# Layer 0's gate and up projections by seven products of halves, with weight factors in quarter units

## The chip, the cores and the metric

The kernel runs on one core of a Trainium2 chip. The metric is device time in microseconds (us), the median of several executions; less is better. The engines of the core are named PE (TensorE, matmuls), DVE (VectorE), ACT (ScalarE), POOL (GpSimd) and SP (SyncE, which here only issues DMAs).

## What is computed

Two layers of a latent transformer-like block on 512 latent tokens and 256 context tokens, width 1024, all in float32. Cut to what matters here:

```python
for l in range(2):
    mod = silu(c) @ w_mod[l] + b_mod[l]            # six vectors of 1024, also for the context
    p = (rmsnorm(x) * (1 + sc1) + sh1) @ w_in[l] + b_in[l]
    y = concat(mlstm_bidir(p), chunk_sgu(p), conformer_conv(p))
    x = x + g1 * (y @ w_out[l])
    h = rmsnorm(x) * (1 + sc2) + sh2
    gate, up = split(h @ w_gu[l])                  # 1024 -> 2 x 2816
    x = x + g2 * ((silu(gate) * up) @ w_down[l])   # 2816 -> 1024
    # the context takes the same path in layer 0; in layer 1 it only feeds the mLSTM states
return rmsnorm(x) * final_g
```

So layer 0's feed-forward part (FFN) works on 768 tokens, layer 1's on 512.

## The kernel before

Everything stands with features on the 128 partitions and tokens along the free dimension. A float32 product is made from two rounded parts of each operand: `hi` is the value cast to the matmul's float32 format (ACT), `lo` the rest (DVE), and one slice of a product is three matmuls, hi by hi, hi by lo and lo by hi (lines 453 to 455 for plain columns). Activations stand split in HA (512 latent tokens) and HB (256 context tokens). A column is one 128-wide piece of an output; for gate and up it has 8 slices of the inner dimension.

**What sets the order.** The program is written as Python generators, one for each little job. A planner, class `Plan`, gives each engine's instructions an order: it advances the generator that can start first by its costs, and by priority where several can. A generator yields an engine's cost, an event to wait for (`W`), or a request for buffers (`A`), and `release` gives them back. The resulting order on each engine is fixed in the program. PE's own order of weight columns is the list `steps`; `ORDER` lists the weights in the same order, `loader()` issues their DMAs on SP one after the other into four `raw` buffers of 512 KB, and `splitter()` makes hi and lo of each, in the same order, in five `spl` buffers. Ten `slot` buffers hold the attention's work and the FFN's hidden activations. `spread(a, b)` mixes the steps of b evenly among those of a.

**FFN of layer 0, before.** All 22 hidden pieces j have a gate and an up column, both plain: for each, 8 slices times three matmuls for the 256 context tokens and for the 512 latent tokens. `gu_evac` makes silu(gate) * up and splits it. The down projection runs in three groups of hidden pieces (8, 7 and 7, `FFN_GROUPS`), each adding to the residual xT (`resid`, line 823). The modulation vectors of layer 1 (and one of layer 0) are summed on DVE among these steps (`modh_steps`, lines 644 and 647), 512 KB of weights at a time.

**FFN of layer 1, before.** Two pieces j are plain (`NPLAIN`). The other 20 are done in pairs by seven products of halves (Winograd's form of Strassen's algorithm): gate and up weights are cut in halves of the inner dimension, the tokens in two halves too (HM = 256), and seven products of four slices replace eight. The sums of weights are made in place in `raw` by `pair_sums` (lines 343 to 376): casts on ACT (line 350), low parts (354) and sums (359) on DVE. The factors of tokens are made once by `t_forms` (lines 1733 to 1751), before the first pair's second product. `pair_steps` and `pair_end` give PE's order, `product` (1783 to 1785) the matmuls, `copy_out`, `join_one` and `pair_out` take the results from PSUM. A whole weight pair takes three `spl` buffers and one of two small `u4` buffers, which stand in a part of HA that is free once the plain columns end. Columns of the down projection are mixed among the pairs four blocks behind each group.

Of the kernel before, what the change touches and what calls it, by code (L numbers as in the profile page):

```python
# [14 lines left out]
P = 128  # L15
D = 1024
KD = 8
# [17 lines left out]
FFN_GROUPS = (((0, 8), (8, 7), (15, 7)), ((0, 6), (6, 6), (12, 5), (17, 5)))  # L35
NPLAIN = 2
# [181 lines left out]
BUFFERS = {"ps": 8, "slot": 10, "raw": 4, "spl": 5, "hp": 0, "u4": 0, "pb": 4, "wi": 3, "cp": 1, "kk": 2, "hc": 2, "C0": 5, "C1": 5}  # L218
# [3 lines left out]
def backbone(ctx, tc, xT_d, cT_d, wmod_d, wb_d, wgv_d, wv_d, wout_d, wgu_d, wd_d, sw_d, sb_d, cv_d, rv_d, id_d, mk_d, out_d):  # L222
# [21 lines left out]
    HA = pers.tile([P, 2, KD, NX], F32R, name="HA")  # L244
    HB = pers.tile([P, 2, KD, NC], F32R, name="HB")
# [56 lines left out]
    def loader():  # L302
        for i, key in enumerate(ORDER):
# [5 lines left out]
            if key[0] == "gp":  # L309
                if key[3] == 0:  # L310
                    rs = []
# [6 lines left out]
                    RAW[key[:3]] = rs  # L318
                    fire(ev("raw", key[:3]), DMA_LAT)
                continue  # L320
# [16 lines left out]
    def take_spl(i):  # L337
        SPL[i] = (buf("hi", [P, KD, P], "hi", F32R), buf("lo", [P, KD, P], "lo", F32R))
        return SPL[i]

    U4 = []

    def pair_sums(key, us):

        r1, r2 = RAW.pop(key[:3])
        a11, a12, a21, a22 = r1[:, 0:4], r1[:, 4:8], r2[:, 0:4], r2[:, 4:8]

        def cast(u, x):
            yield ACT(x.shape[1] * P)
            act.copy(us[u][0], x)  # L350

        def low(u, x):
            yield DVE2(x.shape[1] * P)
            dve.tensor_tensor(us[u][1], x, us[u][0].bitcast(F32), ALU.subtract)
            fire(ev("w", INDEX[key[:3] + (u,)]))

        def add(o, x, y):
            yield DVE2(4 * P)
            dve.tensor_tensor(o, x, y, ALU.add)

        yield from cast(0, r1)
        yield from cast(3, a22)
        yield from low(0, r1)
        yield from low(3, a22)
        yield from add(a22, a21, a22)
        yield from add(a21, a11, a21)
        yield W(ev("u", key[:3], 1))
        yield from cast(1, r2)
        yield from add(a11, a22, a11)
        yield from add(a12, a11, a12)  # L370
        yield W(ev("u", key[:3], 2))
        yield from cast(2, r1)
        yield from low(1, r2)
        release("raw")
        yield from low(2, r1)
        release("raw")

    def split_pair(i, key):
        u, us = key[3], USET.setdefault(key[:3], {})
        if u == 3:  # L380
            return
        yield A("spl")
        us[u] = take_spl(i)
        if u:
            fire(ev("u", key[:3], u))
            return
        yield A("u4")
        us[3] = SPL[INDEX[key[:3] + (3,)]] = U4.pop(0)
        yield W(ev("raw", key[:3]))
        spawn(pair_sums(key, us), 0)  # L390

    USET = {}

    def splitter():
        for i, key in enumerate(ORDER):
            if key[0] == "x":
                continue
            if key[0] == "gp":
                yield from split_pair(i, key)
                continue  # L400
            yield W(ev("raw", i))
            if key[0][:3] == "mod":
                SPL[i] = RAW.pop(i)
                fire(ev("w", i))
                continue
            _, a, b = wsrc(key)
            yield A("spl")
            hi = buf("hi", [P, a, b], "hi", F32R)
            lo = buf("lo", [P, a, b], "lo", F32R)
            SPL[i] = (hi, lo)  # L410
            yield ACT(a * b)
            act.copy(hi, RAW[i])  # L412
            spawn(split_lo(i, hi, lo), 0)
# [22 lines left out]
    def tiles(items, lead, lag, nk, src, wait=None, order=None, depth=3, wide=False, mid=None, after=None, ahead=2):  # L436
# [8 lines left out]
        def mm(i, g, p, j, k):  # L445
# [3 lines left out]
            hi, lo = ws[i]  # L449
# [7 lines left out]
        def close(i, g, p):  # L457
            left[i] = left.get(i, len(groups)) - 1
            if left[i] == 0:
                release("spl")  # L460
# [163 lines left out]
    def modh_steps(l, v):  # L624
        toks = (0, 1) if l == 0 or v < 2 else (0,)

        def work(half, k2, s):
            if k2 == 0:
                mod_acc[l, v, half] = [None, 0, set()]
                yield A("slot")  # L630
                mod_acc[l, v, half][0] = slot([P, 2, 512], "macc")
# [4 lines left out]
            for i in range(2):  # L636
                k = 2 * k2 + i
                for g in toks:
# [3 lines left out]
                    if first:  # L642
                        yield DVE1P(512)
                        dve.tensor_scalar(a[:, g, :], s[:, i, :], c, None, ALU.mult)
                    else:
                        yield STT(512)
                        dve.scalar_tensor_tensor(a[:, g, :], s[:, i, :], c, a[:, g, :], ALU.mult, ALU.add)  # L647
# [7 lines left out]
            for i, g in enumerate(toks):  # L655
                for c in range(4):
                    pe.matmul(p[32 * c:32 * c + 32, 0:P], lhsT=esel[:, g, :], rhs=a[:, g, c * P:(c + 1) * P],
                              start=(i == 0), stop=(i == len(toks) - 1), skip_group_check=True)
            release("slot")
# [182 lines left out]
    def layer(l):  # L842
# [796 lines left out]
        if last:  # L1639
            steps.append(([], lambda: spawn_ffn()))  # L1640
        steps += tiles([out_col(d) for d in range(KD)], gl, gg, KD, hsrc, lambda k, g: E("ys", g["t0"], k), YK, wide=True, ahead=AHEAD[1])

        hid, gups = {}, {}

        def spawn_ffn():
# [3 lines left out]
            yield  # L1649

# [10 lines left out]
        def hid_slot(j):  # L1661
            if j not in hid:
                hid[j] = None
                if last:
                    yield W(E("ffnmem"))
                    yield A("hp")
                    hid[j] = st["hp"].pop(0)
                else:
                    yield A("slot")
                    x = slot([P, 2, T], "hid", F32R)  # L1670
                    hid[j] = (x[:, 0], x[:, 1])
# [3 lines left out]
        def hid_free(js):  # L1675
            if last:
                st["hp"] += [hid[j] for j in js]
                release("hp", len(js))
# [422 lines left out]
```

## Time and profile before

| | |
|---|---|
| median of 3 runs | 1569.57 us (1568.96 to 1571.85) |
| the profiled execution | 1569.28 us; its span 1567.5 us |
| PE busy | 1525.9 us (97%), 10472 matmuls |
| DVE busy | 966.2 us (62%) |
| ACT busy | 590.3 us (38%) |
| granted PE clock, mean | 0.994 |
| bytes read from HBM | 169.34 MB, 109 GB/s over the span |

In the profile, L453 is line 453 of the kernel. Matmuls overlap, so their mean durations are longer than the distance from one start to the next. A window's row gives its length, then for each engine the busy time and (in brackets) the number of instructions, the granted clock, the busy share of the DMA engines and GB/s. A row of the timeline gives start, duration, engine, line, operation, and the count of instructions merged.

### The profile page before, as it was taken

How to read it: one execution, taken by the hardware profiler on the slowest of the kernel's cores; microseconds unless marked ns; L12 is line 12 of the kernel's file. 1: busy time of each engine (PE TensorE's matmuls, PEld its weight loads, DVE VectorE, ACT ScalarE, POOL GpSimd, SP SyncE). 2: the span in 40 equal slices, each digit the busy share in tenths (PEclk: the TensorE clock that was granted, in tenths of full speed). 3: DMA queues.
4: the chain of work that ended last, by engine and by line, in shares of the span. 5: the costliest groups of instructions: out<-in, count | busy, mean ns of one | idle time of the engine just before them, and what ended most of it. 6: DMA issues, size and time to landing. Idle time of an engine off the chain costs nothing.

```text
span 1567.5 us, 25687 instructions
## 1 busy us (share of the span) xinstructions
PE 1525.9 (97%) x10472; PEld 1360.0 (87%) x10472; DVE 966.2 (62%) x1934; ACT 590.3 (38%) x1128; POOL 30.9 (2%) x50
## 2 busy tenths in 40 slices
PE   4999999999999999999999999999999799999997
PEld 3887888888888888888888888878999799999997
DVE  4449877456655555433444345496777886776775
ACT  4332267543322211221122234415664454443443
POOL 0000011000000000000000000000000000000000
PEclk9999999999999999999999999999999899999999
DMA  9434344312243334433343211322331133233331
GB/s 325 150 111 140 106 131 149 141 54 82 81 136 121 110 105 136 134 120 101 130 148 109 93 62 62 102 76 88 115 109 55 55 121 95 96 101 102 105 111 55
DMA packets 69362, 173.21 MB, mean 111 GB/s; under 512 B 7180, under 2 KB 18556, under 8 KB 69244
## 3 DMA queue, kind: packets, MB, share of 16 engines
q1 hardware_dynamic: 66476, 170.16, 33.1%
q8 instruction: 82, 1.34, 0.3%
q10 hardware_dynamic: 2768, 1.42, 0.3%
q14 instruction: 36, 0.29, 0.1%
HBM read 169.34 MB, written 2.21 MB: 109 GB/s over the span
## 4 chain that ended last, share of the span: by engine, by line
PE 94%; DVE 3%; DMA 1%; ACT 1%; issue 1%; SPq 0%; POOLq 0%; POOL 0%; DVEq 0%; ACTq 0%
PE mm L453 23%; PE mm L454 22%; PE mm L455 22%; PE bA L1785 2%; PE bA L1783 2%; PE bA L1784 2%; PE vp L1224 2%; PE vp L1226 1%; PE vp L1225 1%; PE bC L1785 1%; PE bC L1783 1%; PE bC L1784 1%; PE stp L1361 1%; PE num L1445 1%; PE num L1448 1%; PE modps L575 1%
## 5 line engine op out<-in xcount | busy, mean ns | idle before, releaser
L453 PE MATMUL mm<-HA,hi 128*128 128x512 f32 (+1 forms) x928 | 347.0, 374 | 1.7 <-ACT HA L1523 1.2
L454 PE MATMUL mm<-HA,hi 128*128 128x512 f32 (+1 forms) x928 | 337.9, 364 | 1.3 <-DVE HA L790 1.0
L455 PE MATMUL mm<-HA,lo 128*128 128x512 f32 (+1 forms) x928 | 337.4, 364 | 0.0
L412 ACT CAST hi<-raw 128x1024 fp32r<-128x1024 f32 (+5 forms) x170 | 165.9, 979 | 406.4 <-PE mm L454 148.3
L333 DVE TENSOR_TENSOR lo<-raw,hi 128x1024 fp32r<-128x1024 f32 (+5 forms) x170 | 192.5, 1135 | 159.9 <-ACT hi L412 151.9
L453 PEld LDWEIGHTS mm<-HA,hi 128*128 128x128 f32 x928 | 175.1, 189 | 31.4 <-issue 4.7
L455 PEld LDWEIGHTS mm<-HA,lo 128*128 128x128 f32 x928 | 174.5, 188 | 29.9
L454 PEld LDWEIGHTS mm<-HA,hi 128*128 128x128 f32 x928 | 175.0, 189 | 25.8 <-DVE HA L790 1.9
L453 PE MATMUL mm<-HB,hi 128*128 128x256 f32 x592 | 170.1, 287 | 0.0
L823 DVE SCALAR_TENSOR_TENSOR xT<-mm,modc,xT 128x256 f32<-128x256 f32 (+1 forms) x144 | 77.4, 542 | 146.3 <-PE mm L455 145.5
L454 PE MATMUL mm<-HB,hi 128*128 128x256 f32 x592 | 165.0, 279 | 0.8 <-DVE HB L790 0.8
L455 PE MATMUL mm<-HB,lo 128*128 128x256 f32 x592 | 164.8, 278 | 0.0
L453 PE MATMUL mm<-hid,hi 128*128 128x256 f32 (+1 forms) x352 | 119.6, 340 | 0.0
L453 PEld LDWEIGHTS mm<-HB,hi 128*128 128x128 f32 x592 | 111.3, 188 | 8.8 <-issue 5.4
L455 PE MATMUL mm<-hid,lo 128*128 128x256 f32 (+1 forms) x352 | 118.7, 337 | 0.0
L454 PE MATMUL mm<-hid,hi 128*128 128x256 f32 (+1 forms) x352 | 118.4, 336 | 0.0
L454 PEld LDWEIGHTS mm<-HB,hi 128*128 128x128 f32 x592 | 112.2, 190 | 3.8 <-DVE HB L790 1.0
L455 PEld LDWEIGHTS mm<-HB,lo 128*128 128x128 f32 x592 | 111.3, 188 | 0.0
L647 DVE SCALAR_TENSOR_TENSOR macc<-raw,csil,macc 128x512 f32<-128x512 f32 x140 | 101.6, 746 | 0.7
L454 PE MATMUL mm<-ffn,hi 128*128 128x256 f32 x352 | 99.1, 282 | 0.3 <-DVE ffn L1886 0.3
L453 PE MATMUL mm<-ffn,hi 128*128 128x256 f32 x352 | 99.1, 281 | 0.1
L455 PE MATMUL mm<-ffn,lo 128*128 128x256 f32 x352 | 98.4, 280 | 0.0
(302 smaller groups left out, 2993.7 us busy)
## 6 DMA issues: line engine op xcount, KB each, us to landing
raw<-in_wmod SPq DMA_DIRECT2D x96, 512.0 KB, 3.7
raw<-in_wgu SPq DMA_DIRECT2D x88, 512.0 KB, 3.5
raw<-in_wb SPq DMA_DIRECT2D x36, 512.0 KB, 3.5
pbt<-dr SPq DMA_DIRECT2D x40, 256.0 KB, 3.6
raw<-in_wout SPq DMA_DIRECT2D x16, 512.0 KB, 3.5
raw<-in_wd SPq DMA_DIRECT2D x16, 448.0 KB, 3.9
raw<-in_wd SPq DMA_DIRECT2D x16, 384.0 KB, 3.3
raw<-in_wd SPq DMA_DIRECT2D x16, 320.0 KB, 3.0
```

The costliest lines, as they stand in the source:

```text
L333: dve.tensor_tensor(lo, r, hi.bitcast(F32), ALU.subtract)
L412: act.copy(hi, RAW[i])
L453: pe.matmul(o, lhsT=hi[:, k, :], rhs=hh, start=(j == 0), stop=False)
L454: pe.matmul(o, lhsT=hi[:, k, :], rhs=hl, start=False, stop=False)
L455: pe.matmul(o, lhsT=lo[:, k, :], rhs=hh, start=False, stop=(j == nk - 1))
L575: pe.matmul(p[32 * c:32 * c + 32, 0:256], lhsT=csil[:, k, :], rhs=s[:, c, :], start=(k == 0), stop=(k == KD - 1), skip_group_check=True)
L647: dve.scalar_tensor_tensor(a[:, g, :], s[:, i, :], c, a[:, g, :], ALU.mult, ALU.add)
L823: dve.scalar_tensor_tensor(x, p[:, 0:n], MODC[l][:, v, d, g:g + 1], x, ALU.mult, ALU.add)
L1224: pe.matmul(out, lhsT=hh, rhs=hi[:, kk, :], start=(k == 0), stop=False)
L1783: pe.matmul(o, lhsT=hi[:, k], rhs=rh[:, k], start=start and k == 0, stop=False, skip_group_check=True)
L1784: pe.matmul(o, lhsT=hi[:, k], rhs=rl[:, k], start=False, stop=False, skip_group_check=True)
L1785: pe.matmul(o, lhsT=lo[:, k], rhs=rh[:, k], start=False, stop=k == 3, skip_group_check=True)
```

## The change

- **Layer 0 uses pairs too.** `NPLAIN` becomes (2, 2). The 768 tokens are cut in halves of 384, which no longer agree with the norm's groups (512 and 256); HA and HB become views of one tile HH. The first two pieces stay plain.
- **Quarter units.** For pairs and all down groups but the last, the `spl` buffers are taken apart by `to_units` into units of hi and lo for 512 x 128 weights, two from each, and put together again by `from_units` for the last down group. `spl` goes from five to four buffers, so there are eight units for everything. Each of the seven weight factors of a pair takes one unit, in the order in which PE uses them (`PAIR` and the steps' keys); a product gives its unit back when its matmuls end. The `u4` buffers go.
- **Forms by slice.** `t_forms` makes the four token factors for one pair of slices (k, k+4) at a time, as soon as these are normed, and a product waits slice by slice. `spawn_ffn` is asked for after the out columns.
- **Down projection.** Layer 0: six groups (4, 4, 4, 4, 3, 3) for the three, each over the two halves of 384 tokens; all but the last are mixed into two pair blocks each (`D_BLOCKS`). `resid_half` adds to xT, cut where a half crosses the norm's groups.
- **Memory.** `slot` goes from 10 to 12 buffers; the FFN takes all twelve, for forms and hidden pieces. Two of six hidden pieces of layer 0 (`hh`) stand in a quarter of HH that no product reads.
- **Modulation.** Sixteen of the 56 pieces of `modh_steps` move from layer 0's FFN into the later half of its attention and its out columns (`early`); the other forty stay in the FFN and sum in `wi` buffers.
- **Splitter.** It now starts a job for each weight instead of waiting for each load in turn.

```diff
-FFN_GROUPS = (((0, 8), (8, 7), (15, 7)), ((0, 6), (6, 6), (12, 5), (17, 5)))
-NPLAIN = 2
+FFN_GROUPS = (((0, 4), (4, 4), (8, 4), (12, 4), (16, 3), (19, 3)), ((0, 6), (6, 6), (12, 5), (17, 5)))
+NPLAIN = (2, 2)
+D_BLOCKS = (2, 4)
+PAIR = ("a11", "a22", "s4", "s1", "s2", "a12", "s3")
...
-BUFFERS = {"ps": 8, "slot": 10, "raw": 4, "spl": 5, "hp": 0, "u4": 0, "pb": 4, "wi": 3, "cp": 1, "kk": 2, "hc": 2, "C0": 5, "C1": 5}
+BUFFERS = {"ps": 8, "slot": 12, "raw": 4, "spl": 4, "hp": 0, "hh": 0, "un": 0, "pb": 4, "wi": 3, "cp": 1, "kk": 2, "hc": 2, "C0": 5, "C1": 5}
...
+    def to_units():
+        for b in range(BUFFERS["spl"]):
+            yield A("spl")
+            hi, lo = buf("hi", [P, KD, P], "hi", F32R), buf("lo", [P, KD, P], "lo", F32R)
+            for h in range(2):
+                UN.append((hi[:, 4 * h:4 * h + 4], lo[:, 4 * h:4 * h + 4], b))
+            release("un", 2)
...
+    def split_unit(i, unit, x, then=None):
+        hi, lo = unit[0][:, 0:x.shape[1]], unit[1][:, 0:x.shape[1]]
+        yield ACT(x.shape[1] * P)
+        act.copy(hi, x)
+        yield DVE2(x.shape[1] * P)
+        dve.tensor_tensor(lo, x, hi.bitcast(F32), ALU.subtract)
+        if then is not None:
+            then()
...
+        part("a11", a11)
+        part("a12", a12)
+        yield from add(a21, a21, a22)
+        part("s1", a21)
+        yield seen("a11")
+        yield from add(a11, a21, a11)
+        part("s2", a11)
+        yield seen("s1")
+        yield from add(a21, a11, a22, ALU.subtract)
...
+        part("s3", a21, second)
+        part("a22", a22, second)
+        yield seen("a12")
+        yield seen("s2")
         yield from add(a12, a11, a12)
+        part("s4", a12, lambda: release("raw"))
...
+        def ffn_memory():
+            yield A("slot", 12)
...
+            def form(k, f):
+                for g in (gl, gg):
+                    for kk in (k, k + 4):
+                        yield W(ev("h", l, 1, g["t0"], kk))
+                if k >= 2:
+                    yield W(E("T", k - 2))
...
+                yield DVE2(4 * HM)
+                dve.tensor_tensor(f.rearrange("p a b t -> p a (b t)"), rows[0].bitcast(F32), rows[1].bitcast(F32), ALU.add)
...
+                yield ACT(4 * HM)
+                act.copy(hi, ff)
+                yield DVE2(4 * HM)
+                dve.tensor_tensor(lo, ff, hi.bitcast(F32), ALU.subtract)
+                fire(E("T", k))
...
+            return out + [([key + ("s1",)], fifth), ([key + ("s2",)], sixth), ([key + ("a12",)], second), ([key + ("s3",)], seventh)]
...
+            return [([("gp", l, j, "a22")], fourth), ([("gp", l, j, "s4")], third)]
...
+        if not last:
+            early = [m for v in (5,) for m in modh_steps(l, v)] + modh_steps(l + 1, 1)
+            late = first + (len(steps) - first) // 2
+            steps = steps[:late] + spread(steps[late:], early)
+        steps.append(([], lambda: spawn_ffn()))
...
+            nb = min(D_BLOCKS[l], len(blocks) - b0)
+            for b in range(nb):
+                part = ds[b * len(ds) // nb:(b + 1) * len(ds) // nb]
...
+            steps = steps[:nfirst] + spread(steps[nfirst:], [m for v in (0, 2, 3, 4, 5) for m in modh_steps(l + 1, v, "wi")])
```

More of the change, by code (lines that the diff above doesn't have):

```diff
@@ L378, in split_pair, with __init__, __getitem__ @@
[L378 to L392, printed above, removed]
+    class Parts:
+        def __init__(self, parts):
+            self.parts = parts
+        def __getitem__(self, at):
+            return self.parts[at[1] // 4][:, at[1] % 4, at[2]]
@@ L394, in splitter, with as_is, split @@
+    def as_is(i):
+        yield W(ev("raw", i))
+        SPL[i] = RAW.pop(i)
+        fire(ev("w", i))
+    def split(i, key):
+        _, a, b = wsrc(key)
+        hi = buf("hi", [P, a, b], "hi", F32R)
+        lo = buf("lo", [P, a, b], "lo", F32R)
+        yield W(ev("raw", i))
+        SPL[i] = (hi, lo)
+        yield ACT(a * b)
+        act.copy(hi, RAW[i])
+        yield from split_lo(i, hi, lo)
     def splitter():
+        in_units = set()
         for i, key in enumerate(ORDER):
@@ L434, in hk, with tiles @@
         return lambda k: (a[:, 0, k, o:o + n], a[:, 1, k, o:o + n])
-    def tiles(items, lead, lag, nk, src, wait=None, order=None, depth=3, wide=False, mid=None, after=None, ahead=2):
+    def tiles(items, lead, lag, nk, src, wait=None, order=None, depth=3, wide=False, mid=None, after=None, ahead=2, back=lambda w: release("spl")):
         order = range(nk) if order is None else order
@@ L1651, in gu_col, with plain_done, more_room @@
+        def plain_done():
+            spawn(more_room(), 0)
+            return
+            yield
+        def more_room():
+            for k in range(4):
+                yield W(E("tread", k))
+            more_hid([tuple(HH[:, w, 2 * i:2 * i + 2, HM:2 * HM] for w in range(2)) for i in range(2)], "hh" if not last else "hp")
         def gu_col(i):
@@ L1780, in product @@
+        def product(p, w, right, start):
+            hi, lo = w[0:2]
             o = p[:, 0:HM]
             for k in range(4):
+                if isinstance(right, int):
+                    yield W(E("T", k))
+                    rh, rl = (x[:, right] for x in TF[k])
+                else:
+                    rh, rl = (quarter(w_, *right)[:, k] for w_ in range(2))
                 yield PE(HM, 3)
-                pe.matmul(o, lhsT=hi[:, k], rhs=rh[:, k], start=start and k == 0, stop=False, skip_group_check=True)
@@ L1947, in layer @@
-        steps.extend(d_run(gi))
+                    if final_group:
+                        if not last:
+                            release("slot", 4)
+                    else:
+                        for j in range(j0, j0 + nj):
+                            more_hid([hid[j]], hid_kind(j))
+            lead, lag = (HALF[1], HALF[0]) if not last else HALF
+            back = {} if final_group else dict(back=lambda w: give(w[2]))
+            return tiles([d_col(d) for d in range(KD)], lead, lag, nj, src, lambda k, h: E("hid", j0 + k, h["th"]),
+                         depth=1, wide=final_group, after=after, ahead=AHEAD[3], **back)
@@ new lines, in t_free @@
+        def t_free():
+            if not last:
+                release("slot", 8)
+            return
+            yield
+        if not last:
+            early = [m for v in (5,) for m in modh_steps(l, v)] + modh_steps(l + 1, 1)
+            late = first + (len(steps) - first) // 2
+            steps = steps[:late] + spread(steps[late:], early)
+        steps.append(([], lambda: spawn_ffn()))
+        np_ = NPLAIN[l]
+        steps += tiles([gu_col(i) for i in range(2 * np_)], gl, gg, KD, hsrc, lambda k, g: ev("h", l, 1, g["t0"], k), wide=True, ahead=AHEAD[2])
```

486 lines of the change are left out of this document (259 added, 227 removed).

## The prediction

> **What bounds the kernel now.** I read the busy shares first, then the forty slices, the chain that ended last, then stage windows, and last the groups and the timeline of the stages that change.
>
> ```profile
> span 1567.5 us, 25687 instructions
> PE 1525.9 (97%) x10472; PEld 1360.0 (87%) x10472; DVE 966.2 (62%) x1934; ACT 590.3 (38%) x1128; POOL 30.9 (2%) x50
> PE   4999999999999999999999999999999799999997
> DVE  4449877456655555433444345496777886776775
> PE 94%; DVE 3%; DMA 1%; ACT 1%; issue 1%; SPq 0%; POOLq 0%; POOL 0%; DVEq 0%; ACTq 0%
> 385.00:955.00 570.00, 570.00 (x3409) 492.69 (x3408) 282.46 (x432) 129.94 (x203) 2.88 (x3) 1.00 0.34 113
> 1219.00:1236.00 17.00, 7.29 (x48) 6.31 (x48) 16.97 (x22) 10.98 (x15) 0.00 (x0) 0.76 0.03 5
> 1290.00:1400.00 110.00, 109.94 (x945) 109.74 (x945) 81.98 (x130) 49.36 (x74) 0.00 (x0) 1.00 0.32 103
> ```
>
> In the window rows the columns are length, then busy time of PE, weight load, DVE, ACT, POOL, and the clock. TensorE is the bound: 94% of the chain, and layer 0's FFN (385 to 955) has it busy all 570.00 us with DVE at 282.46. The one weak spot, a 7 among the 9s of PE's slices, is 1219 to 1236, where layer 1 begins its own seven-product pairs: PE 7.29 of 17 us, DVE 16.97. The profiled execution took 1569.28 us (span 1567.5 and 1.8 around it), 0.29 under the median of 1569.57. My sum starts from 1569.28.
>
> **The change part by part.**
>
> *1. Seven products in layer 0.* The pace of matmuls is start to start, since busy times overlap.
>
> ```profile
> 394.75 0.39 PE L453 MATMUL mm<-HA,hi 128*128 128x512 f32 x1
> 411.55 0.28 PE L453 MATMUL mm<-HB,hi 128*128 128x256 f32 x1
> 414.27 0.39 PE L453 MATMUL mm<-HA,hi 128*128 128x512 f32 x1
> L453 PE MATMUL mm<-HA,hi 128*128 128x512 f32 x352 | 140.3, 399 | 0.0
> L453 PE MATMUL mm<-hid,hi 128*128 128x512 f32 x176 | 70.2, 399 | 0.0
> ```
>
> From 394.75 to 411.55 stand three columns of 24 matmuls with 512 tokens: 16.80/72 = 0.2333 us. From 411.55 to 414.27 stand 24 with 256: 0.1133. The 352 are 44 columns of 8 slices, on one of three lines. A pair (gate and up) is now 48 matmuls of each shape: 48 x 0.3466 = 16.64 us. After, it is 7 products x 4 slices x 3 = 84 matmuls of 384 tokens, a shape that no row has. In proportion to the 256 row it is 0.1700, to the 512 row 0.1750; on the straight line between them 0.1733, which I take. 84 x 0.1733 = 14.56, so 2.08 saved in each of 20 pairs: -41.6. The down projection goes from 528 matmuls of each shape to 1056 of 384: 183.0 before and after. At the ends: 0.1700 gives -47.2 and -3.5 = -50.7; 0.1750 gives -38.8 and +1.8 = -37.0.
>
> The Trainium skill ("TensorE: Matmul & The Clock Gate", Back-to-back issue gap) has N/2.4 + 2.5 ns: 162.5 ns at 384, by which the two parts would save 71. Our 512 row is 233 where it has 216, so the trace disagrees.
>
> *2. DVE work in layer 0.* Its paces, again start to start:
>
> ```profile
> 389.84 2.06 DVE L813 SCALAR_TENSOR_TENSOR nt<-xT,gs,rstdb 128x512 f32<-128x512 f32 x3 [1.41 <-PE rstdb L766]
> ...
> 401.08 0.74 DVE L790 SCALAR_TENSOR_TENSOR HA<-nt,modc,HA 128x512 fp32r<-128x512 f32 x1
> 401.74 2.73 DVE L647 SCALAR_TENSOR_TENSOR macc<-raw,csil,macc 128x512 f32<-128x512 f32 x4
> 1200.03 0.48 DVE L790 SCALAR_TENSOR_TENSOR HA<-nt,modc,HA 128x256 fp32r<-128x256 f32 x1
> 1200.42 0.42 DVE L701 TENSOR_TENSOR acc<-acc,sq 128x256 f32<-128x256 f32 x1
> 1200.76 0.47 DVE L813 SCALAR_TENSOR_TENSOR nt<-xT,gs,rstdb 128x256 f32<-128x256 f32 x1
> 1211.14 1.22 DVE L1733 TENSOR_TENSOR tf<-HA 128x1024 f32<-128x1024 f32 x1
> 1222.84 2.35 DVE L354 TENSOR_TENSOR lo<-raw,hi 128x1024 fp32r<-128x1024 f32 x2
> 1225.11 1.29 DVE L354 TENSOR_TENSOR HA<-raw,HA 128x512 fp32r<-128x512 f32 x2
> 1226.31 2.49 DVE L359 TENSOR_TENSOR raw<-raw 128x512 f32<-128x512 f32 x4
> L647 DVE SCALAR_TENSOR_TENSOR macc<-raw,csil,macc 128x512 f32<-128x512 f32 x140 | 101.6, 746 | 0.7
> L359 DVE TENSOR_TENSOR raw<-raw 128x512 f32<-128x512 f32 x80 | 54.4, 686 | 1.0
> L333 DVE TENSOR_TENSOR lo<-raw,hi 128x1024 fp32r<-128x1024 f32 x52 | 63.6, 1222 | 54.6 <-ACT hi L412 53.9
> L823 DVE SCALAR_TENSOR_TENSOR xT<-mm,modc,xT 128x512 f32<-128x512 f32 x24 | 18.0, 750 | 65.0 <-PE mm L455 65.0
> ```
>
> Two-tensor work of 1024 elements: (1225.11 - 1222.84)/2 = 1.135; of 512: (1226.31 - 1225.11)/2 = 0.60; of 256: 1200.76 - 1200.42 = 0.34. With a scalar operand: 401.74 - 401.08 = 0.66 for 512, 1200.42 - 1200.03 = 0.39 for 256. Estimates from these: 384 elements 0.47 and 0.53, 1536 elements 1.67, 128 with a scalar 0.27.
> - Weights of a pair: 7 low parts and 4 sums of 512 = 6.6, before 2 x 1.135 = 2.27: +87 over 20 pairs.
> - Leaving PSUM, a pair: five of 0.47 and two of 0.53 = 3.4, before 0.60 + 0.34 twice = 1.9: +30.
> - Down weights: 8 of 1024 and 16 of 896 (1.0) = 25; after 32 of 512 and 16 of 384 = 27: +2. Residual sums, six groups for three and a half cut where the norms' groups meet: 48 x (0.53 + 0.27 + 0.39) = 57, before 24 x 1.05 = 25: +32.
> - Forms of the tokens: for each of four slices 2 x 1.67 + 2 x 0.47 + 2 x 0.53 = 5.34: +21.4.
> - 16 modulation pieces of four 0.66 leave for the attention: -42.
>
> 282 + 130 = 412 us of 570 - 42 + 16 = 544, or 76%. Layer 1's pairs run at 81.98 of 110 (75%) with PE at 109.94, so on average DVE does not become the bound; ACT had 129.94 of the 570 and would have to double to be half busy. What costs is where the DVE work is bunched.
>
> *3. Start of layer 0's pairs.* The rows at 401 show DVE done with the last normed slice at 401.74, after working without a break since 389.84. PE has four plain columns of 512 from 394.75: 96 x 0.2333 ends at 417.15; the first product (needs no form) ends at 419.2. The second needs all four forms. DVE after 401.74: forms 21.4, one plain column pair 1.2, and the factors that go first by priority, eight units: 8 low parts and 4 sums, 7.2. That is 431.5, and the product ends at 432.0 where it would have at 421.3: PE waits 10.7. If four units go first it is 7; with a late modulation piece (2.6) or an ACT gap behind the copies 16. Before, nothing waited here, so this is a new cost. In the like place of layer 1 the clock fell:
>
> ```profile
> 1219.82 2.00 ACT hi L350 x2
> 1228.80 1.14 DVE HB L1741
> 1233.48 1.15 DVE lo L354
> 1234.67 0.58 PE bC L1785
> 1235.25 0.22 PE bC L1783
> 1255.96 1.23 DVE lo L354
> ```
>
> After the wait a 256-token matmul takes 0.22 instead of 0.1133 for some 3 us: +1.5. Together +12.2 (7 to 18). The same page of the skill (The HAM clock gate) says that one idle window of about 3.4 us halves the clock and as much work restores it; the 0.76 above agrees, and the rule speaks against this change, in the 1.5 already counted.
>
> *4. The first pairs.* A pair without down columns has 14.56 of PE; DVE 6.6 + 3.4 = 10.0, and the modulation pieces left (40 over some 220 steps, 1.3 in a pair's seven, the first eight with four 0.66 each) 3.4. With 13.4 of 14.56 there is little to pay back with, and the two loads of a pair wait in SP's order behind modulation pieces that hold one of four raw buffers until DVE, at lowest priority, has read them:
>
> ```profile
> SPq L327 <- DVE lo L333: 385.8, 94, 22.8
> SPq L327 <- DVE macc L647: 123.4, 49, 15.6
> ```
>
> Now these waits are hidden behind columns that are loaded far ahead. I count +4 (0 to 12). Slots for hidden pieces are few (six), but a group's come free when its last column ends and are asked for three products (36 x 0.1733 = 6.2 us) later: 0 while that cover holds, and what is left of the wait if not.
>
> *5. Layer 0 to layer 1.* The last down group has 3 slices where it had 7.
>
> ```profile
> 931.78 0.40 PE L453 MATMUL mm<-hid,hi 128*128 128x512 f32 x1
> 937.54 0.48 DVE L790 SCALAR_TENSOR_TENSOR HB<-nt,modc,HB 128x256 fp32r<-128x256 f32 x1
> 947.26 0.28 PE L453 MATMUL mm<-HB,hi 128*128 128x256 f32 x1
> ```
>
> PE ends the context group's last column at 931.78 and its first normed slice is there at 938.0, 6.2 us later, under 15.5 us of other columns. After, three columns of 9 x 0.1733 = 4.7 us cover it: 1.5 late, and then the slices come at 2 x 0.39 while PE asks for one in 0.68 and DVE also has the residuals of the other half: +4 (1 to 8).
>
> *6. Layer 1's pairs.* Before, their first factors are cast only at 1219.82, when the plain columns end; after, units come free two columns (5.4 us) earlier and forms go slice by slice. DVE from 1211.14 (its last normed slice done): forms 4 x (2 x 1.135 + 2 x 0.34 + 2 x 0.39) = 14.9, plain columns 8 x 0.34 = 2.7, units 7.2: 1235.9, against 1237.2 where the product with the first form ended (1234.67 + 12 matmuls at 0.21). DVE still bounds it: -1.2 (-6 to +3). In the steady part the weights of a pair go from 3 x 1.135 + 5 x 0.60 = 6.4 us of DVE to 11 x 0.60 = 6.6; eight units stand ahead where five buffers and two quarters made twelve halves, and the one wait of before (1255.96, some 1.7) may recur: with the fifth split buffer gone in the attention, +1.5 (0 to 8).
>
> *7. Moved modulation.* 42 us of DVE go into the later half of layer 0's attention, where its slices read 4 to 7: hidden, and if not, the chain of the chunks is late: +2 (0 to 6). Bytes are the same; 24 more, smaller issues on SP wait for buffers anyway: 0. POOL's queue is not touched: 0.
>
> **Sum.** -41.6 + 12.2 + 4 + 4 - 1.2 + 1.5 + 2 = -19.1: 1550.2, say 1550.
>
> **The rivals.**
> - *Cheaper* (0.12). 384 tokens at 0.1700 (-50.7), the start waits 7 + 1.5, the rest 5: 1532. For it: 256 is as near to 384 as 512 is. Against: the same, from the other end.
> - *The skill's gap* (0.04). A pace that has no extra per column: -71 + 20 gives 1518. Every row here is over it.
> - *DVE late in every pure pair* (0.17). With durations that do not overlap (512: 0.686 in the groups) a pair's DVE work is 11 x 0.686 + 7 x 0.55 + 3.9 = 15.3, over PE's 14.56, and layer 1's short look-ahead adds the like: 10 to 18 more, 1560 to 1568. Against: the overlap is in every timeline row.
> - *Raw buffers* (0.10), the other side. If each of 20 pair heads waits the 2.5 us that SP's wait for macc lasts on average (123.4/49), 50 us come in place of the 4: 1596. It decides from (1569.3 - 1550.2 + 4)/20 = 1.2 us a pair. For it: four buffers, a pair holds two. Against: a pair's loads lead by more than one pair's 14.56.
>
> **How the numbers follow.** Forecast 0.57 (1541 to 1561), cheaper 0.12, the skill's gap 0.04, DVE late 0.17, raw buffers 0.10. A change of 0.2% (3 us) is what a measurement of this kernel can tell. Faster: 0.57 + 0.16 + 0.12 of DVE late = 0.85; same 0.06; slower 0.09. The range 1533 to 1568 leaves out the skill's gap, part of the cheaper case and the raw buffers, under 2 in 10.
>
> **What would show it.** 384-token matmuls some 0.173 apart in the timeline; a dip in PE's slices near 420 with DVE full and a clock under 1.00; the 7 near 1219 less deep or the same; PE waits on HB at the layer change; DVE about 75% in layer 0's FFN. I am wrong if the 384 pace is not between 0.170 and 0.175, or if waits of PE on low parts or on raw loads recur in every pair.

## The result, and the profile after

The changed kernel takes 1579.76 us (median of 4 runs, 1579.14 to 1581.47) against 1570.09 for the kernel before beside it: a ratio of 1.0062 [1.0045, 1.008] (in brackets, here and below, the 95% interval). It is slower by 0.6%, where 1550 was forecast. Its profiled run took 1579.2 us, with a span of 1577.4, 9.9 over the span before.

Totals, slices and the chain of the page, the kernel after:

```profile
span 1577.4 us, 26171 instructions
PE 1502.8 (95%) x10232; PEld 1398.8 (89%) x10232; DVE 1147.4 (73%) x2416; ACT 678.1 (43%) x1402; POOL 33.3 (2%) x50
...
PE   5999999999789999999999989999999799999997
...
DVE  5359889777977876767777774687768876777765
...
PEclk9999999999989999999999989999999899999999
...
PE 90%; DVE 5%; DMA 2%; ACT 1%; issue 1%; POOL 0%; SPq 0%; POOLq 0%; DVEq 0%; ACTq 0%
```

PE is busy for 23 us less than before, and the span is still longer: PE waits more. Three dips stand where one stood: at 0.27 of the span (the start of layer 0's pairs), at 0.6 (the layer change) and at 0.79 (the start of layer 1's pairs). The clock dips at the same places.

To see where the time went I cut the span at points that both kernels have: the sums of squares (stat) that close a stage, and layer 1's first gate product (gvp). Rows of the timeline, the kernel before (L751 is stat, L889 gvp):

```profile
385.03 0.94 PE L751 MATMUL stat<-onesD,acc 128*128 128x1 f32 x8
...
951.01 0.94 PE L751 MATMUL stat<-onesD,acc 128*128 128x1 f32 x8
...
982.40 0.28 PE L889 MATMUL gvp<-HB,hi 128*16 128x256 f32 x1
...
1193.34 0.50 PE L751 MATMUL stat<-onesD,acc 128*128 128x1 f32 x4
...
1557.78 0.38 PE L751 MATMUL stat<-onesD,acc 128*128 128x1 f32 x2
```

and the kernel after (L831 and L969):

```profile
390.46 0.95 PE L831 MATMUL stat<-onesD,acc 128*128 128x1 f32 x8
...
940.60 1.70 PE L831 MATMUL stat<-onesD,acc 128*128 128x1 f32 x8
...
977.58 0.28 PE L969 MATMUL gvp<-HH,hi 128*16 128x256 f32 x1
...
1191.03 0.50 PE L831 MATMUL stat<-onesD,acc 128*128 128x1 f32 x4
...
1567.71 0.38 PE L831 MATMUL stat<-onesD,acc 128*128 128x1 f32 x2
```

| stage | before | after | difference | forecast |
|---|---|---|---|---|
| up to layer 0's FFN | 385.0 | 390.5 | +5.4 | +2 |
| layer 0's FFN | 566.0 | 550.1 | -15.8 | -41.6 +12.2 +4, and part of the layer change |
| layer 1's norm and first columns | 31.4 | 37.0 | +5.6 | the rest of the layer change (+4 in all) |
| layer 1's attention | 210.9 | 213.4 | +2.5 | in the +1.5 |
| layer 1's FFN | 364.4 | 376.7 | +12.2 | -1.2 +1.5 |

The differences are taken from the rows before rounding, and add to the 9.9. Two amounts in them are work that only moves from one stage to the next. The moved modulation takes 64 small matmuls from layer 0's FFN into the first stage; 16 of them take 0.57 us (379.05 to 379.62), so 2.3 us. And of layer 1's context columns the kernel before has 33 matmuls done ahead of the stat at 951.01, the kernel after 6 ahead of the one at 940.60: 27 x 0.1133 = 3.1 us now stand behind it, so that of the +5.6 only 2.5 is lost time.

Windows of the kernel after; the columns are those of the prediction's window rows:

```profile
390.50:940.60 550.10, 525.44 (x3028) 510.91 (x3027) 410.42 (x737) 206.09 (x384) 2.08 (x2) 0.97 0.32 102
445.00:902.00 457.00, 453.25 (x2654) 446.53 (x2653) 333.26 (x604) 165.74 (x319) 0.00 (x0) 1.00 0.35 109
904.00:941.00 37.00, 30.31 (x163) 28.76 (x162) 29.04 (x60) 17.57 (x31) 1.07 (x1) 0.89 0.34 107
...
1290.00:1400.00 110.00, 108.35 (x918) 108.15 (x917) 80.77 (x154) 49.69 (x99) 0.00 (x0) 1.00 0.33 99
...
427.50:444.50 17.00, 5.77 (x15) 4.11 (x14) 15.27 (x24) 5.60 (x8) 0.00 (x0) 0.50 0.07 17
933.00:946.00 13.00, 9.45 (x40) 8.78 (x41) 8.75 (x22) 5.84 (x11) 2.25 (x2) 0.50 0.18 53
```

Layer 0's pairs themselves, 445 to 902, have PE busy for 453 of 457 us at full clock: there the change does what was forecast. The losses of this stage stand at its two edges: 17 us at half clock behind 427, of which PE is busy for 5.8, and 13 us at half clock round 940.

What PE waited for, in the kernel after: at the start (420 to 445), in layer 0's pairs (445 to 902) and in layer 1's (1240 to 1535). The columns are total, times, longest:

```profile
PE bC L1887 <- ACT ffn L1794: 7.7, 3, 4.0
PE bC L1888 <- DVE ffn L1796: 6.6, 3, 3.0
...
PE mm L530 <- DVE lo L376: 2.1, 1, 2.1
PE bA L1887 <- ACT x L1958: 1.6, 4, 0.6
...
PE bC L1887 <- DVE d L1962: 6.6, 4, 1.6
```

The first two rows are the token forms, slice by slice (L1794 casts the high part on ACT, L1796 subtracts the low part on DVE). The last is new in layer 1: four times a pair's last product (bC) waits until DVE has joined d, that is, added bC to the copy of bA.

### The profile page after: what moved, and what is told of

Read it like the earlier page. It is cut to its first block, busy times and chain, and to the rows that moved or that the text cites. A ratio compares the mean times of both kernels' runs of the same rounds, so it can differ in the third digit from the quotient of the medians.

```text
span 1577.4 us, 26171 instructions
## 1 busy us (share of the span) xinstructions
PE 1502.8 (95%) x10232; PEld 1398.8 (89%) x10232; DVE 1147.4 (73%) x2416; ACT 678.1 (43%) x1402; POOL 33.3 (2%) x50
## 4 chain that ended last, share of the span: by engine, by line
PE 90%; DVE 5%; DMA 2%; ACT 1%; issue 1%; POOL 0%; SPq 0%; POOLq 0%; DVEq 0%; ACTq 0%
PE mm L528 15%; PE mm L529 15%; PE mm L530 15%; PE bA L1887 6%; PE bA L1888 6%; PE bA L1889 6%; PE bC L1887 3%; PE bC L1888 3%; PE bC L1889 3%; PE vp L1304 2%; PE vp L1305 1%; PE vp L1306 1%; PE bB L1887 1%; PE bB L1889 1%; PE bB L1888 1%; PE stp L1441 1%
## 5 line engine op out<-in xcount | busy, mean ns | idle before, releaser
L528 PE MATMUL mm<-HH,hi 128*128 128x256 f32 (+2 forms) x1008 | 342.3, 340 | 2.9 <-ACT HH L1603 1.7
L529 PE MATMUL mm<-HH,hi 128*128 128x256 f32 (+2 forms) x1008 | 329.3, 327 | 2.6 <-DVE HH L870 2.3
L530 PE MATMUL mm<-HH,lo 128*128 128x256 f32 (+2 forms) x1008 | 329.0, 326 | 0.9 <-DVE lo L334 0.9
L374 ACT CAST hi<-raw 128x512 fp32r<-128x512 f32 (+3 forms) x368 | 214.5, 603 | 215.1 <-PE mm L529 47.5
L376 DVE TENSOR_TENSOR lo<-raw,hi 128x512 fp32r<-128x512 f32 (+3 forms) x368 | 236.7, 663 | 67.1 <-ACT hi L374 64.4
L528 PEld LDWEIGHTS mm<-HH,hi 128*128 128x128 f32 x1008 | 191.6, 190 | 24.0 <-issue 8.0
L530 PEld LDWEIGHTS mm<-HH,lo 128*128 128x128 f32 x1008 | 191.4, 190 | 16.2 <-DVE lo L334 1.3
L529 PEld LDWEIGHTS mm<-HH,hi 128*128 128x128 f32 x1008 | 191.9, 190 | 14.9 <-DVE HH L870 3.3
L530 PE MATMUL mm<-ffn,lo 128*128 128x256 f32 (+1 forms) x576 | 176.3, 306 | 2.1 <-DVE lo L376 2.1
L528 PE MATMUL mm<-ffn,hi 128*128 128x256 f32 (+1 forms) x576 | 177.1, 307 | 0.7 <-ACT ffn L2006 0.5
L529 PE MATMUL mm<-ffn,hi 128*128 128x256 f32 (+1 forms) x576 | 176.5, 306 | 0.5 <-DVE ffn L2001 0.3
L1888 PE MATMUL bA<-ffn,hi 128*128 128x384 f32 (+1 forms) x480 | 149.2, 311 | 0.0
L528 PEld LDWEIGHTS mm<-ffn,hi 128*128 128x128 f32 x576 | 108.5, 188 | 2.3 <-ACT ffn L2006 0.8
L529 PEld LDWEIGHTS mm<-ffn,hi 128*128 128x128 f32 x576 | 108.4, 188 | 1.0 <-DVE ffn L2001 0.5
```

Source lines behind the costliest of these rows:

```text
L374: act.copy(hi, x)
L376: dve.tensor_tensor(lo, x, hi.bitcast(F32), ALU.subtract)
L528: pe.matmul(o, lhsT=hi[:, k, :], rhs=hh, start=(j == 0), stop=False)
L529: pe.matmul(o, lhsT=hi[:, k, :], rhs=hl, start=False, stop=False)
L530: pe.matmul(o, lhsT=lo[:, k, :], rhs=hh, start=False, stop=(j == nk - 1))
L1888: pe.matmul(o, lhsT=hi[:, k], rhs=rl, start=False, stop=False, skip_group_check=True)
```

## The experiments

My theory after the first reading: four separate losses, each from work that stands in DVE's queue or from a cover that became short. (a) The start of layer 0's pairs waits for the forms. (b) The last down group is too short for the DVE work that hangs on its end. (c) In layer 1 the join of d queues behind a low part that itself waits for the product before. (d) The modulation pieces moved into the attention are not hidden. Rivals: the new layout of the tokens slows PE; the split buffer given up costs look-ahead; at the layer change it is only DVE's order.

**The start.** plain3 gives layer 0 one more plain pair.

```
-NPLAIN = (2, 2)
+NPLAIN = (3, 2)
```

> Layer 0 keeps three plain hidden pieces instead of two (NPLAIN = (3, 2)), so PE has 16.6 us more of work that needs no token form before the first pair; its price is one pair less: 16.64 - 14.6 = 2.1 us. Theory (the bunch of DVE work at the start of layer 0's pairs is paid once): the waits of 18.2 us between 420 and 445, half clock in them included, go nearly all; 1579.8 - 18.2 + 2.1 = 1564, 1562 to 1567. Rival (DVE stays behind, because the pairs leave it no time to catch up): the wait comes back in the next pairs and the time is 1574 or more.

1568.12 us, ratio to before 0.9997 [0.9987, 1.0007]: 10 (by the ratios) to 12 us (by the medians) under the change, 1 us above the theory's range and far from the rival's. The window of plain3 over the place where the change idles:

```profile
423.00:445.00 22.00, 22.00 (x105) 19.04 (x105) 19.84 (x31) 10.51 (x19) 0.00 (x0) 1.00 0.08 20
```

The same window in the kernel after has PE busy for 7.78 us, at a clock of 0.61. DVE is as full in both; only what PE has to do meanwhile differs. A wait of 14.3 us plus half clock is replaced by a plain pair that costs 2.08 us more than seven products. In its own stage the trace gains 13.8 us (392.18 to 928.49, from stat to stat, is 536.3 for 550.1). That it is not 16 goes with new waits in the pairs (plain3, 395 to 945); the rest is that this profiled run came to the stage 1.7 us later, with nothing changed before it:

```profile
PE bA L1887 <- ACT x L1958: 5.0, 4, 1.4
...
PE bA L1887 <- ACT d L1958: 1.9, 1, 1.9
```

**Layer 1's join.** join lets the copy and the join of d go ahead of weight splitting.

```
-                spawn(copy_out(j, 2), 0.6)
+                spawn(copy_out(j, 2), -0.5)
```

> Only the planner's priority of the sum d + C in both layers is raised above the weight splits (from 0.6 to -0.5). Theory (in layer 1's pairs PE waits four times 1.81 us for d, which stands in DVE's queue behind the low part of a unit that PE itself frees only with the product before): these waits go and the time falls by 6 to 8, 1572 to 1574. Rival (DVE has no time left in pairs without down columns, 8.9 of 9.55 us, so another product waits instead): within 3 us of 1579.8.

1572.24 us, 1.0024 [1.0015, 1.0033], some 7 under the change: the theory held. None of the L1962 waits is left in layer 1's pairs. The loop in the timeline of the kernel after, first case:

```profile
1254.45 0.28 PE L1889 MATMUL bA<-HH,lo 128*128 128x256 f32 x1
1254.65 0.62 ACT L374 CAST hi<-raw 128x512 fp32r<-128x512 f32 x1 [0.40 <-PE bA L1888]
1254.68 1.30 DVE L376 TENSOR_TENSOR lo<-raw,hi 128x512 fp32r<-128x512 f32 x2
...
1255.91 0.41 DVE L1962 TENSOR_TENSOR d<-d,bC 128x256 f32<-128x256 f32 x1
1256.37 0.39 PE L1887 MATMUL bC<-HH,hi 128*128 128x256 f32 x1 [1.65 <-DVE d L1962]
```

The product before (bA) frees a weight unit; ACT casts the next factor into it; DVE subtracts its low part, and the join, ready long before, stands behind that in DVE's queue. PE waits for the join. No engine is full: of the 50 us from 1250 to 1300, in which three of the four waits stand, PE is busy for 45.06, DVE for 38.47 and ACT for 25.72. It is a ring of queues with a fixed order, closed by the eight units.

**The layer change.** last6 makes layer 0's last group six slices. Its pieces 16 and 17 stand where layer 1's normed tokens are written meanwhile, so that the down product reads changed values; the amount of work is the same.

```
-FFN_GROUPS = (((0, 4), (4, 4), (8, 4), (12, 4), (16, 3), (19, 3)), ((0, 6), (6, 6), (12, 5), (17, 5)))
+FFN_GROUPS = (((0, 4), (4, 4), (8, 4), (12, 4), (16, 6)), ((0, 6), (6, 6), (12, 5), (17, 5)))
```

> Layer 0's last two down groups (3 and 3 slices) become one of 6, so three columns after the context's last one cover 3 x 18 x 0.174 = 9.4 us where they covered 4.7. Theory (the change of layer costs some 15 us because the last group is too short to hide the chain residual - square - sum - norm, 6.2 us long before): most of it goes, 1566 to 1571. Rival (DVE's order is at fault: it splits the next layer's weights ahead of the residuals whatever the group's length): less than 4 us go, 1576 to 1580.

1576.62 us, 1.0047 [1.0032, 1.0062]: about 3 under the change. By its time the rival's range held. At the layer change itself, though, nearly everything goes: PE's waits from 930 to 985 fall from 6.1 to 2.1 us, the one for stat from 3.2 to 0.2, and the clock from 895 to 985 is 1.00 for 0.92. The pairs wait 6.2 us for x, where it was 1.6, which hides most of that gain. So two more runs. resfirst changes only the priority of the last group's residuals, squares and sums:

```
-                return (("d", l, gi, d), evac, 0.5)
+                return (("d", l, gi, d), evac, -1 if final_group and not last else 0.5)
```

> The kernel after; only the residual sums and squares behind the last down group of layer 0 go ahead of everything else on DVE, in front of the low parts of layer 1's first weights. Theory (at the layer change the 3.2 us wait for the last sum of squares comes from four low parts of 1024 elements, 1.2 us each, that DVE takes first): the wait for stat shrinks by 2 to 3 us, and with it the half-clock period; 1574 to 1577. Rival (the last group of 3 slices is too short a cover whatever DVE's order): 1579 to 1580.

1578.35 us, 1.006 [1.0048, 1.0073]: within the noise as the change, between the two ranges and nearer to the rival's. The wait only moves on to the next sum:

```profile
PE stat L831 <- DVE acc L781: 4.1, 2, 2.2
PE rstdb L846 <- POOL rs L264: 2.0, 1, 2.0
```

The edit did not reach the order that its theory speaks of. In its trace low parts of 1.2 us still begin at 932.49 and 935.23, ahead of the last sum of the context's squares at 936.36, because ACT makes the squares for it late, at 935.47, right behind a weight cast (934.52, 1.04 us). So this run tells that the priority alone does not help; whether another order on ACT and DVE together would is not shown.

last4 gives the last group four slices, with nothing overwritten:

```
-FFN_GROUPS = (((0, 4), (4, 4), (8, 4), (12, 4), (16, 3), (19, 3)), ((0, 6), (6, 6), (12, 5), (17, 5)))
+FFN_GROUPS = (((0, 4), (4, 4), (8, 4), (12, 3), (15, 3), (18, 4)), ((0, 6), (6, 6), (12, 5), (17, 5)))
```

> The kernel after, with layer 0's down groups (0,4) (4,4) (8,4) (12,3) (15,3) (18,4): the last group has four slices in place of three; the work is the same. Theory (the layer change is late because three columns of the other half are too short a cover for the norm's chain): the cover goes from 3 x 9 x 0.1733 = 4.7 us to 6.2 us, so the waits at the layer change lose 1.5 us and the half-clock period perhaps one window of it: 1576 to 1578.5. Rival (the cover does not matter, since the chain begins and ends with the last column whatever its length): 1579 to 1580.

1576.17 us, 1.0042 [1.0027, 1.0057]. Its layer-0 FFN is 5.7 us shorter than the change's:

```profile
391.07 0.95 PE L831 MATMUL stat<-onesD,acc 128*128 128x1 f32 x8
...
935.55 1.70 PE L831 MATMUL stat<-onesD,acc 128*128 128x1 f32 x8
```

The time is in the theory's range, and the waits for stat are gone. What is late in the change, rows of its timeline:

```profile
930.02 1.22 DVE L334 TENSOR_TENSOR lo<-raw,hi 128x1024 fp32r<-128x1024 f32 x1
...
931.56 1.22 DVE L334 TENSOR_TENSOR lo<-raw,hi 128x1024 fp32r<-128x1024 f32 x1
...
933.23 0.41 DVE L781 TENSOR_TENSOR acc<-acc,sq 128x256 f32<-128x256 f32 x1
933.69 1.01 PE L831 MATMUL stat<-onesD,acc 128*128 128x1 f32 x4 [3.17 <-DVE acc L781]
...
938.83 0.47 DVE L870 SCALAR_TENSOR_TENSOR HH<-nt,modc,HH 128x256 fp32r<-128x256 f32 x1
```

The context's last column ends on PE at 925.7 and its first normed slice is there at 939.3, 13.6 us later; in the kernel before this chain took 6.2. In the last group's 37 us (904 to 941, above) DVE is busy for 29.04, and PE's own work is 144 x 0.1736 = 25.0. The residuals, the squares, layer 1's first low parts and its norm hang on the end of the group whatever its length; in the kernel before the last group had 56 x 3 x 0.3466 = 58.2 us of PE to hide them. Each of the last columns is now 9 x 0.1736 = 1.56 us of PE and brings DVE a low part, a residual and a sum, at the paces of the prediction 2.0 to 2.3 us (1.14, 0.53 and 0.34 to 0.60), so by this estimate DVE falls behind there. With four slices a column is 2.08. (Whether the sum of that DVE work or the length of the chain behind the last column counts more, last4 does not say: it helps both.)

**The moved modulation.** late16 takes the 16 pieces that the change moved into layer 0's attention back among the FFN's pairs, where all 56 then stand.

```
-            early = [m for v in (5,) for m in modh_steps(l, v)] + modh_steps(l + 1, 1)
+            early = []
...
-            steps = steps[:nfirst] + spread(steps[nfirst:], [m for v in (0, 2, 3, 4, 5) for m in modh_steps(l + 1, v, "wi")])
+            steps = steps[:nfirst] + spread(steps[nfirst:], modh_steps(l, 5, "wi") + [m for v in (1, 0, 2, 3, 4, 5) for m in modh_steps(l + 1, v, "wi")])
```

> The sixteen modulation pieces stay in layer 0's FFN, as before the change, so all 56 are mixed among its pairs. Theory (they cost the attention 5.5 us, 2.4 of it their 64 matmuls that only move): the first stat of the latent group comes at 386 to 388 instead of 390.5, the attention gains 3 us, and the 42 us of DVE work hide among the pairs, as DVE was at 75% there; 1575 to 1580. Rival (DVE has no room at the start of the pairs): the start's waits grow by 5 to 10 us, 1582 to 1588.

1583.39 us, 1.0093 [1.0078, 1.0108]: in the rival's range, but not for the rival's reason, since the waits for the forms at the start are 14.5 us for 14.3. The attention gives back 6.9 us (390.46 to 383.56 below), more than the 5.4 lost, and layer 0's FFN takes 8.3 more (558.4 for 550.1), 2.3 of them for the matmuls that come back:

```profile
383.56 0.95 PE L831 MATMUL stat<-onesD,acc 128*128 128x1 f32 x8
...
941.95 1.70 PE L831 MATMUL stat<-onesD,acc 128*128 128x1 f32 x8
```

So the pieces do cost in the attention, and cost more in the FFN: the change's place for them is the better of the two, by some 4 us. What else they cost in the FFN stays open.

**Layout, look-ahead and pace.** In layer 1 the 256-token matmuls come 118 ns apart after and often 114 before; over some 2900 of them in its FFN the mean distance is 117.8 ns after and 116.5 before, which makes 3.8 us. Twelve of one product, first and last row (before; after):

```profile
1403.45 0.28 PE L1783 MATMUL bB<-HA,hi 128*128 128x256 f32 x1
...
1404.71 0.28 PE L1785 MATMUL bB<-HA,lo 128*128 128x256 f32 x1
```

```profile
1412.22 0.28 PE L1887 MATMUL bB<-HH,hi 128*128 128x256 f32 x1
...
1413.52 0.28 PE L1889 MATMUL bB<-HH,lo 128*128 128x256 f32 x1
```

1.26/11 = 114.5 ns against 1.30/11 = 118.2. b_hh is the kernel before with the tokens in one buffer, as the change has them.

```
-    HA = pers.tile([P, 2, KD, NX], F32R, name="HA")
-    HB = pers.tile([P, 2, KD, NC], F32R, name="HB")
+    HH = pers.tile([P, 2, KD, T], F32R, name="HH")
+    HA, HB = HH[:, :, :, 0:NX], HH[:, :, :, NX:T]
...
```

> The kernel before, with its latent and context tokens as two views of one buffer of 768 columns, as in the kernel after; nothing else changed. Theory (where a matmul's moving operand stands sets its pace): 256-token matmuls of layer 1's seven products that read tokens, 114 ns apart in the trace of before, go to 118 as in the trace of after; about 1260 of them x 3.5 ns = +4.4 us in layer 1's FFN, while the 512-token ones of layer 0 go from 233 to 230 ns and its 256-token ones from 114 to 118, about cancelling. Time before +3 to +5: 1572 to 1574. Rival (the pace belongs to the new way of keeping weight factors): no change, 1569 +- 1.5, and 114 ns stay.

1569.34 us, 1.0 [0.9991, 1.0009], and the pace stays 114 (1.25/11; the mean over layer 1's FFN is 116.4):

```profile
1404.17 0.28 PE L1781 MATMUL bB<-HH,hi 128*128 128x256 f32 x1
...
1405.42 0.28 PE L1783 MATMUL bB<-HH,lo 128*128 128x256 f32 x1
```

My theory fell: the layout is not it. tfhb therefore keeps the change and puts the first two token forms wholly into the context's place and the last two into slots, as before; the casts and low parts of a slice's forms are cut in two accordingly:

```
-                    TF[k] = (HB[:, k // 2, 4 * (k % 2):4 * (k % 2) + 4, :], flat[k][:, 0:1024].rearrange("p (k t) -> p k t", k=4))
+                    for w in range(2):
+                        TF[k, w] = (HB[:, w].rearrange("p (r k) t -> p r k t", r=2)[:, :, k], flat[2 * w + k // 2][:, 0:1024].rearrange("p (r k t) -> p r k t", r=2, k=2)[:, :, k % 2])
...
```

> The kernel after; in layer 1 the first two token forms stand wholly in the context tokens' place (as in the kernel before) and the last two wholly in slots, so that each product's moving operands come from one place; before this edit each product read its high parts from the one and its low parts from the other. Eight casts and eight low parts of 1024 become sixteen of 512. Theory (the 256-token pace keeps 113 ns through products that read tokens or the context's place alone, and 118 where a slot is mixed in): five of seven products at 113 to 114, 19 pairs x 60 x 4 ns = -4.6 us, +1 at the start: 1575.5 to 1577. Rival (the pace is set by something else, such as the units of weights): 118 stays, 1579.5 to 1581.

1582.38 us, 1.0089 [1.0075, 1.0103]; the same twelve rows, from 1414.08 to 1415.38, are 118.2 ns apart. This theory fell too, and the time is above both ranges; that the additional instructions cost the 2.6 us is a guess. b_spl4 is the kernel before with four split buffers.

```
-"spl": 5
+"spl": 4
```

> The kernel before with four split buffers for weights in place of five, as in the kernel after. Theory (the lost look-ahead is part of what layer 1's attention and FFN lost): before +1 to +4, 1570 to 1573, with new waits of PE on low parts of weights. Rival (the fifth buffer was never needed, and layer 1's loss is the order of queues and the pace): 1569 +- 1.

1597.14 us, 1.0177 [1.0164, 1.0191]: far over both theories. All of it is in layer 1's pairs (b_spl4, 1222 to 1535):

```profile
PE bC L1785 <- DVE lo L354: 18.8, 12, 3.2
PE bC L1783 <- ACT hi L350: 3.8, 1, 3.8
```

The row of L354 was 4.1 us, once, in the kernel before. Its attention and layer 0 are as before (layer 1's attention 210.2 for 210.9). So in the kernel before the fifth buffer carried layer 1's look-ahead. The change has four as well and no such waits in its pairs; its four of 1.6 us are for d and go with join. That its smaller units make up for the buffer is my reading, since no run changes the units alone. The buffer is not what the attention lost; nor is the layout (211.1 in b_hh).

**Do the gains add?** p3join is plain3 with join.

> The kernel after with three plain pairs in layer 0 in place of two (plain3) and with the copy and join of a pair's d ahead of weight splitting (join). Theory (the two losses have separate causes, in layer 0's start and in layer 1's pairs): the gains of the two runs add, 11.6 + 7.5 less what was counted twice: 1560 to 1563. Rival (the copies that go first hold back weight factors in layer 0, where three plain pairs left new waits in the pairs): 1565 to 1569.

1559.47 us, 0.994 [0.9927, 0.9954]: they add, and the kernel is now 0.6% faster than before. p33join has three plain pairs in layer 1 too (`NPLAIN = (3, 3)`).

> p3join with three plain pairs in layer 1 too. Theory (the start of layer 1's pairs waits for the token forms as layer 0's did, 10.9 us of idle PE at 1215 to 1224 and half a clock behind it): one more plain pair costs 96 x 0.1175 - 84 x 0.1175 = 1.4 us and covers most of that: 6 to 10 us faster than p3join, 1550 to 1554. Rival (layer 1's weight factors, not its forms, are late at the start: DVE is full there and a plain pair adds DVE work): 1557 to 1561.

1554.49 us, 0.9907 [0.9892, 0.9923]: 5.0 us, a little less than expected, since waits for the forms of 3.4 us (9.2 in p3join) and a smaller clock dip stay. p3jlast4 is p3join with last4's groups.

> p3join with last4's down groups. Theory: the gain of last4, if there is one, adds: 1556 to 1558. Rival: new waits on slots for hidden pieces in the pairs, as in last6, take it back: 1559 to 1562.

1551.79 us, 0.9889 [0.9875, 0.9903]: 7.7 us, more than the 3.6 of last4 alone and beyond both ranges. The waits of the pairs for x fall too, from 6.1 to 2.3 us. p33jlast4 has all four edits.

> The kernel after with three plain pairs in both layers, the copy and join of d ahead of weight splitting, and a last down group of four slices in layer 0. Theory (four separate causes): the gains add, 1551.8 of p3jlast4 less the 5.0 between p33join and p3join: 1546 to 1548. Rival (what one edit gains another had gained already): 1550 to 1552.

1545.47 us, 0.985 [0.9835, 0.9865]: 34 us under the change and 1.5% under the kernel before, slightly below what the sum had promised. Its windows of layer 0's and layer 1's FFN:

```profile
390.00:945.00 555.00, 547.91 (x3206) 532.80 (x3206) 421.35 (x758) 212.33 (x396) 3.84 (x3) 0.99 0.32 101
1171.90:1536.40 364.50, 357.93 (x3000) 356.31 (x2998) 278.91 (x539) 177.56 (x352) 2.09 (x3) 0.99 0.30 89
```

besttf adds tfhb's edit to it.

> p33jlast4 with tfhb's edit. Theory: 1541 to 1544. Rival: 1545 to 1547.

1548.93 us, 0.9869 [0.9856, 0.9883]: above both ranges and slower by 3, as tfhb was. p33jlast4 is the best version.

## Why the prediction was wrong

The forecast of the gain was right and the forecast of its price was wrong: 19 us of net gain expected, 10 us of loss measured. Of these 29 us some 14 lie in layer 1 (step 6), 7 in the layer change (step 5), 6 in the start of the pairs (step 3) and 1 in the moved modulation (step 7). No rival of mine priced one of these losses where it stands (the nearest, "DVE late", put it in every pair), and neither sign that I had named for being wrong showed: the pace at 384 tokens came out and no wait recurs in every pair. The losses stand at the edges of the stages, in four pairs of layer 1 and in the pace at 256.

1. *Seven products, -41.6: right.* 384-token matmuls come 0.1736 us apart (a product in the pairs runs from 629.67 to 631.58 in eleven steps); 0.1733 was forecast.
2. *DVE work, 412 of 544 us: right*, 410.42 of 550.10. That "on average DVE does not become the bound" was right too, and of little use: most of the loss sits where DVE's work is bunched.
3. *Start of the pairs, +12.2 (7 to 18): mis-sized, some 18.* In the timeline of the kernel after, the second product begins at 423.02 and the one behind it at 442.28, where its twelve matmuls take 12 x 0.1736 = 2.1 us: 17.2 late, and 1 more until the clock is back at 444.5.

```profile
423.02 0.34 PE L1887 MATMUL bC<-ffn,hi 128*128 128x384 f32 x1
...
442.28 0.52 PE L1887 MATMUL bA<-ffn,hi 128*128 128x384 f32 x1
```

   From the last normed slice (407.6) to the last form (441.4) DVE does 19.4 us for forms, 9.6 for weight factors, 3.2 for the results of plain columns and 1.5 for modulation; I had counted 7.2, 1.2 and 0 for the last three. The term for the waits was 10.7 and measured 14.3; the term for the clock was 1.5, from layer 1's 3 us at half clock, and measured the other 3.9, with the clock at 0.50 for 17 us. plain3 showed that a plain pair at 2.08 us is the cheaper cover.
4. *First pairs, +4 (0 to 12): the number right by luck.* From 445 to 902 PE waits 3.7 us in all, but none of it for raw loads, which the 4 stood for: 2.1 are for a low part of the down weights, 1.6 for copies out of PSUM. The raw-buffer rival, my only one on the slower side, is refuted; so is "DVE late in every pair" for layer 0.
5. *Layer change, +4 (1 to 8): failed, some 11.* Some 9 stand at the end of layer 0's FFN (10.1 us from the last down matmul to the stat at 940.60, with little more than 1 us of work) and 2.5 behind it. I compared the 4.7 us of cover with the 6.2 us that the chain had taken before, and took that length as fixed. It took 13.6. It was short because DVE had time under the columns of a group of 58 us; under 25 us of PE work the same residuals, squares, low parts and norm queue up. The sum of DVE's work against PE's, made for the FFN as a whole in step 2, was not made for this group and its last columns. last6 and last4 show that the length of the group matters. That no order of the queues would do as well is not shown.
6. *Layer 1, -1.2 + 1.5: the step that failed most, +12.2 in its FFN and +2.5 in its attention.* About 7 of it is the join's loop, which join removed: I counted instructions per pair (6.4 to 6.6 us of DVE) and never followed one unit round from PE to ACT to DVE and back to PE. Some 4 are the pace of 118 ns (2900 matmuls x 1.3 ns); its cause is open. The start, where I had forecast a gain of 1.2, got worse: the waits for the forms are 9.2 us, where the kernel before waited 7.9 for weights. The price I gave to the lost split buffer was too small in itself, as b_spl4's 28 us show, and did not come due. What the attention's 2.5 are was not tried, except that neither the buffer nor the layout makes them.
7. *Moved modulation, +2 (0 to 6): a net 3.1*, the +5.4 less the 2.3 of PE work that the FFN no longer has. In the traces of other kernels with nothing changed up to there the stat comes at 390.4 to 394.4, so this size is uncertain by some us.

Steps 3, 5, 6 and 7 each came out over my value: I gave each edge its own price and each a mild one, though 3, 5 and most of 6 draw on the same queue, DVE's.

## What to carry to other kernels

When a change moves work onto a second engine, make that engine's sum against the first one's for each edge of each stage and not for the stage: the start, the last columns of the last group, and every ring of buffers that passes through both. A smaller last group shortens the cover and leaves all the work that hangs on its end. And look at the length of a chain as something that the change can stretch: from the last column of a group to the first normed slice, 6.2 us became 13.6. Where a consumer waits for a small instruction behind a big one in a queue of fixed order, its place counts more than its length: a join of 0.41 us made PE wait 1.65.

## What was not expected of the hardware

The 256-token pace has two values, 113 to 114 and 118 ns, and keeps one over many columns: in the kernel before, layer 0's columns of 256 tokens run at 113 from 411 to 463 us and at 118 from there to 600. The 512-token ones between them also have two values, 233 and 231, but do not change over with them: they stay at 233 until 540. Layer 1's pairs change over at 1257 and at 1277. From 1300 to 1530 the matmuls whose moving operand stands in a slot run at 118 throughout, and those that read tokens or the context's place at 113.6 or 118, on average at 114.6; in the kernel after all run at 117 to 118. One buffer for all tokens does not do that (b_hh, 114.8), and forms that stand whole in one place do not undo it (tfhb, 117.9). The cause is open. The 512-token matmuls got faster with the change, from 233 to 229 ns in layer 0's attention (200 to 385 us); b_hh keeps 233, so this is not the layout either.

And the granted clock stayed at 0.50 for 17 us at the start of layer 0's pairs, in which PE had 5.77 us of work in pieces (the window above); the forecast had taken 3 us for it from layer 1. Finer windows of the kernel after show the steps. The clock fell at 427.5 after waits of only 1.2 and 1.8 us with one matmul between them, and at 932.6, 2.1 us after the last down matmul. It came back at 444.5, after 3.0 us of nearly unbroken work, and at 946.3, after 6.9.
